# Two-by-two blocks with seven products for the gate and up projections of twenty feature blocks

## The chip, the cores and the metric

One core of one Trainium2 chip runs the whole program. The metric is the device time of one execution in microseconds (us); the kernel before takes 2099.5 us, the median of three runs from 2099.29 to 2100.41 us.

## What is computed

One decoder layer on 1024 tokens of width 1024 in 32-bit floats: a SwiGLU feed-forward of 2816 features, a token mixer (four gated-DeltaNet heads and four gated-linear-attention heads), and a second SwiGLU, each followed by a layer norm. The part that the change touches is the two feed-forwards:

```python
def _swiglu(x, w_gate, w_up, w_down):
    return (jax.nn.silu(x @ w_gate) * (x @ w_up)) @ w_down

x = _layer_norm(ALPHA * x + 0.5 * _swiglu(x, ffn1...), ln1_g, ln1_b)
x = _layer_norm(ALPHA * x + _token_mixer(x, ...), ln2_g, ln2_b)
x = _layer_norm(ALPHA * x + 0.5 * _swiglu(x, ffn2...), ln3_g, ln3_b)
```

## The kernel before, in words

Features are cut into 22 blocks of 128, tokens into two halves of 512, and the width 1024 (over which gate and up sum) into eight slices of 128. Every operand of a large product is kept as two parts, hi and lo (`split`, L120 and L121: ScalarE casts hi, VectorE subtracts to get lo), and each product is three matmuls: hi·hi, hi·lo, lo·hi. So the gate of one block for one half of the tokens (`proj`, L183, L184 and L186) is 8 slices x 3 = 24 matmuls of 128x128 by 128x512 into one PSUM bank. The weights come in two loads of 256 KB per block and matrix (`weight`, L128), into raw tiles `wr` (five of them), and are split into `wh` and `wl` (six pairs).

`hidden` makes a block: gate for each half, Silu on ScalarE (L314), up for each half, the product with the gate on VectorE (L319), and the split of the result. `down` (L205 to L207, L210) multiplies the results of two blocks with their rows of `w_down`: units of one token block of 128 and one half of the columns, 2 x 3 matmuls each into one of three `pd` banks, and VectorE adds the bank to the running sum `acc` in SBUF (L210).

The stages in their order: `ffn_groups(1, ...)` does blocks 0 to 11 of the first feed-forward in pairs for both halves (to about 400 us); inside it `hidden_first` brings in x itself, with `acc` as its staging room, and the constants are loaded after the second pair. `middle` does blocks 12 to 21 of the first feed-forward one half at a time, the first norm, the mixer, the second norm, and blocks 0 to 7 of the second feed-forward, of which half 1 comes last, from about 1500 us. There `ffn` takes the Tanh form of Silu. `ffn_groups(2, ...)` does blocks 8 to 17 in pairs for both halves, and blocks 18 to 21 half by half with the last norm amid them.

All of this is one stream of instructions for each engine. The framework that builds the program puts each engine's instructions in an order of its own, by the order of the text and by when it reckons each to be ready; on the chip each engine then takes its queue in that order. SP issues all loads and stores. The layer norm `ln` (L250 to L257) transposes the rows through `pd`, writes `xf` on ScalarE (L254) and splits it into the parts of x for the next stage.

Of the kernel before, what the change touches and what calls it, by code (L numbers as in the profile page):

```python
# [28 lines left out]
# the rows that the layer norms get here are the reference's over ALPHA  # L29
# [13 lines left out]
BUFS = {"w": 6, "h": 3, "xf": 3, "wr": 5, "f": 4, "g": 6, "raw": 1, "q": 1, "k": 2, "v": 1, "tt": 1, "z": 1, "on": 2, "am": 1, "pt": 1, "qd": 1, "vb": 1,  # L43
        "v0": 1, "v1": 1, "kd": 1, "mi": 1, "ui": 1, "wi": 2}
K1, K2 = 12, 8
LAST = 4
# [35 lines left out]
class Layer:  # L82
    def __init__(self, tc, ctx, a):
        self.tc, self.nc, self.a = tc, tc.nc, a
        pool = lambda name, bufs, **kw: ctx.enter_context(tc.tile_pool(name=name, bufs=bufs, **kw))
        self.cp = pool("cp", 1)
        self.xp = pool("xp", 1)
        self.wp = pool("wp", 1)
        self.sp = pool("sp", 1)
# [6 lines left out]
        self.centred = {}  # L96

# [15 lines left out]

    def xtile(self, half, k):
# [19 lines left out]
    def constants(self):  # L134
        cp, nc = self.cp, self.nc
# [7 lines left out]
        self.mhalf = cp.tile([P, 4], F32, name="mhalf")  # L143
        nc.gpsimd.memset(self.mhalf[:], -0.5)

    def load_constants(self):
# [3 lines left out]
        for j in range(0, MASKW, HT):  # L150
            w = min(HT, MASKW - j)
            raw = self.u("xf", self.wp)
# [8 lines left out]
    def load_x(self, half, k):  # L161
        h, l = self.xtile(half, k)
        c = 4 * half + k // 2
        if k % 2 == 0:
            # acc serves as staging room until it is loaded itself
            self.acc[c] = self.wt(self.xp, [D], f"acc{c}", 1)
# [4 lines left out]
    def load_acc(self, c):  # L171
        t = self.acc[c]
        self.tc.keep_in_program_order(self.nc.sync.dma_start(t[:], self.a["x"][c]))
# [15 lines left out]
    def down(self, hs, ws, half, scale, cs=range(4), sums=None, cuts=((0, HT), (HT, D)), ahead=1):  # L189
        """acc += scale / ALPHA * sum of h w for the half's token blocks cs; sums gets the new acc's sums over the columns."""  # L190
# [3 lines left out]
        while units:  # L194
            # the first few units take all but the last h first, which has just been computed
# [22 lines left out]
    def ln_stats(self, c, cuts=2):  # L218
        nc = self.nc
        acc = self.acc[c]  # L220
        st = self.wt(self.sp, [4, 6], "st", 2)
        mv = self.wt(self.sp, [4], "mv", 3)
# [8 lines left out]
    def ln_row(self, i, d, tags="gb", bufs=1):  # L231
        out = []
        for j in range(2):
            t = self.wt(self.wp, [HT], tags[j], bufs)
# [4 lines left out]
    def ln(self, i, half):  # L239
        """Normalises the half's acc, writes the parts hi and lo of the transpose of LN(acc)."""  # L240
# [5 lines left out]
        for k in range(KB):  # L246
# [6 lines left out]
            xf = self.u("xf", self.wp)  # L253
            nc.scalar.activation(xf[:], ps[:], AF.Identity, bias=bc, scale=gc)  # L254
            self.split(h[:], l[:], xf[:])
# [11 lines left out]
    def out_stats(self, c, sums):  # L267
        """The rows' means and reciprocal deviations; (acc - mean) * g in two temporary tiles."""
# [5 lines left out]
        else:  # L274
            mv, sq = self.wt(self.sp, [4], "mv", 3), self.tiny("sq", 2)
# [11 lines left out]
    def centre(self, c, mv, ds=(0, 1)):  # L287
        for d in ds:
            t = self.centred[c, d] = self.u("xf", self.wp)
# [16 lines left out]
    def gate_silu(self, w, half, tanh):  # L306
        nc = self.nc
        ps = yield from self.proj(w, half)
        s = self.u("xf", self.wp)
# [14 lines left out]
    def hidden(self, idx, f, halves, pool, tags, bufs, tanh=False):  # L324
        """silu(x w_gate) * (x w_up) of one block of features (twice that with tanh), as parts hi and lo."""
# [31 lines left out]
    def ffn(self, idx, fs, half):  # L357
        """The blocks fs of features for one half of the tokens, two at a time."""
        for n in range(0, len(fs), 2):
            hs = []  # L360
            for f in fs[n:n + 2]:
                h = yield from self.hidden(idx, f, (half,), self.wp, ("hh", "hl"), BUFS["h"], True)
                hs.append(h[half])
            ws = [self.weight(self.a[f"wd{idx}"][f]) for f in fs[n:n + 2]]
            yield from self.down(hs, ws, half, 0.25, ahead=AHEAD)

    def ffn_groups(self, idx, groups, first=False, last=()):
        """Blocks of features in groups, both halves of the tokens, while the mixer needs no room."""
        with self.tc.tile_pool(name=self.nm("fx"), bufs=1) as fx:
            for n, fs in enumerate(groups):  # L370
                hs = []
                for f in fs:
                    if first and f == 0:
                        hs.append(self.hidden_first(fx, ("gh", "gl"), BUFS["g"]))
                    else:
                        hs.append(now(self.hidden(idx, f, (0, 1), fx, ("gh", "gl"), BUFS["g"])))
                self.downs_group(idx, fs, hs, (0, 1), fx, first=first and fs[0] == 0)
                if first and n == 1:
                    self.load_constants()
            if last:  # L380
                for half in range(2):
                    hs = [now(self.hidden(idx, f, (half,), fx, ("gh", "gl"), BUFS["g"])) for f in last]
                    self.downs_group(idx, last, hs, (half,), fx, end=True)

    def downs_group(self, idx, fs, hs, halves, fx, first=False, end=False):
        ws = [self.weight(self.a[f"wd{idx}"][f], *((fx, "f") if 2 * n < BUFS["f"] else ())) for n, f in enumerate(fs)]
        if first:
            for c in range(KB):
                self.load_acc(c)
        for half in halves:  # L390
            for c in range(4):
                sums = self.tiny("sums", 2) if end and c < 3 else None
                last = end and half == 1 and c == 3
                work = self.down([h[half] for h in hs], ws, half, 0.5, [c], sums,
                                 ((0, HT), (HT, HT + HT // 2), (HT + HT // 2, D)) if last else ((0, HT), (HT, D)))
                if end:
                    for _ in range(2):
                        next(work)
                    if half or c:
                        self.out_rows(4 * half + c - 1)  # L400
                now(work)
                if end:
                    self.out_stats(4 * half + c, sums)
            if end and half:
                self.out_rows(KB - 1)
# [101 lines left out]
    def finish(self, ons, half, blk, wz, wcol):  # L507
        """Gates heads' normalised outputs [token, dv] and adds their share of w_out."""
        nc = self.nc
        ms = []  # L510
        for n, on in enumerate(ons):
            ps = yield from self.proj(self.weight(self.a["win"][wz + n]), half)
            m = [self.wt(self.wp, [HT], t, BUFS["h"], F32R) for t in ("hh", "hl")]
# [13 lines left out]
    def pull(self, n, skip=0):  # L527
        """Emits about n products of the work that waits, from its entry number skip on."""
# [31 lines left out]
    def gdn(self, h, half, free):  # L560
# [50 lines left out]
        # the inverse of each B0 x B0 diagonal block of I + A, column after column from the last  # L611
# [8 lines left out]
        for j in range(B0 - 1, 0, -1):  # L620
            # row j of each block, in all of the block's partitions
# [14 lines left out]
        for b in LEVELS:  # L636
            # the columns of the second halves of the blocks of 2 * b
# [18 lines left out]
        for b in (32, 64):  # L656
            # block by block, as the halves of the blocks begin at partitions that the engines can start at
# [6 lines left out]
            # over all rows of the block, as the others are zero: all products that write a bank start at the same row  # L664
# [45 lines left out]
    def values(self, ws, half):  # L710
        """The pair's values with the tokens on the partitions: both weights have the columns of both heads, for half of the rows."""
# [47 lines left out]
    def gla(self, p, half, free):  # L759
# [41 lines left out]
        for i, hb in enumerate(GLEVELS):  # L801
# [8 lines left out]
            # the rows of the second halves are masked below, so that any finite numbers serve there  # L810
# [46 lines left out]
    def run(self):  # L857
        self.constants()
        self.halo, self.S, self.SB = {}, [None] * NH, [None] * 2
        self.ffn_groups(1, [range(n, n + 2) for n in range(0, K1, 2)], first=True)  # L860
        with self.tc.tile_pool(name="mp", bufs=1) as self.mp:
            self.middle()
        cut = [*range(K2, NF - LAST, 2), NF - LAST]
        self.ffn_groups(2, [range(a, b) for a, b in zip(cut, cut[1:])], last=range(NF - LAST, NF))

    def middle(self):
# [43 lines left out]
        now(self.ffn(2, range(K2), 1))  # L910
# [69 lines left out]
```

## Time and profile before

| | us |
|---|---|
| median of three runs | 2099.5 |
| span of the profiled execution, first to last instruction | 2097.4 |
| TensorE (PE) busy | 2067.7 |
| VectorE (DVE) busy | 1284.9 |
| ScalarE (ACT) busy | 697.2 |

The profiled execution's own time is its span of 2097.4 us and what lies around it. Against the median this is 2.1 us (2099.5 - 2097.4). In the tables of stretches each engine shows its busy time and, in brackets, the number of its instructions that began there. A matmul's row shows some 0.39 us, but the matmuls overlap: what one costs is the distance between the starts of two.

### The profile page before, as it was taken

How to read it: one execution, taken by the hardware profiler on the slowest of the kernel's cores; microseconds unless marked ns; L12 is line 12 of the kernel's file. 1: busy time of each engine (PE TensorE's matmuls, PEld its weight loads, DVE VectorE, ACT ScalarE, POOL GpSimd, SP SyncE). 2: the span in 40 equal slices, each digit the busy share in tenths (PEclk: the TensorE clock that was granted, in tenths of full speed). 3: DMA queues.
4: the chain of work that ended last, by engine and by line, in shares of the span. 5: the costliest groups of instructions: out<-in, count | busy, mean ns of one | idle time of the engine just before them, and what ended most of it. 6: DMA issues, size and time to landing. Idle time of an engine off the chain costs nothing.

```text
span 2097.4 us, 27456 instructions
## 1 busy us (share of the span) xinstructions
PE 2067.7 (99%) x10292; PEld 1695.0 (81%) x10292; DVE 1284.9 (61%) x2793; ACT 697.2 (33%) x1395; POOL 54.6 (3%) x87
## 2 busy tenths in 40 slices
PE   9999999999999999999999999999999999999998
PEld 7888888888887787788788777888788888888887
DVE  4434333454678888768899887778755333333456
ACT  5211121123254444434464443343422211112232
POOL 0000000000000000000101000001000000000000
PEclk9999999999999999999999999999999999999999
DMA  8111111122222212222131222122323211111232
GB/s 288 49 55 48 43 55 46 46 97 99 89 93 86 71 56 79 70 69 91 66 111 66 71 76 66 66 71 71 121 96 105 80 46 46 51 40 61 76 106 85
DMA packets 87109, 163.03 MB, mean 78 GB/s; under 512 B 10048, under 2 KB 10560, under 8 KB 86976
## 3 DMA queue, kind: packets, MB, share of 16 engines
q1 hardware_dynamic: 86976, 161.29, 22.9%
q8 instruction: 80, 1.31, 0.3%
q14 instruction: 53, 0.43, 0.1%
HBM read 157.06 MB, written 4.19 MB: 77 GB/s over the span
## 4 chain that ended last, share of the span: by engine, by line
PE 87%; DVE 8%; ACT 2%; issue 2%; POOL 1%; DMA 1%; SPq 0%; DVEq 0%; ACTq 0%; POOLq 0%
PE pa L183 17%; PE pa L184 17%; PE pa L186 17%; PE pd L205 8%; PE pd L206 8%; PE pd L207 8%; PE pm L824 1%; PE pm L422 1%; DVE wl L121 1%; DVE acc L210 1%; DVE acc L264 1%; PE pa L724 1%; DVE xl L121 1%; PE pa L725 1%; PE pa L723 1%
## 5 line engine op out<-in xcount | busy, mean ns | idle before, releaser
L183 PE MATMUL pa<-xh,wh 128*128 128x512 f32 x1808 | 716.6, 397 | 8.7 <-ACT xh L120 5.1
L184 PE MATMUL pa<-xl,wh 128*128 128x512 f32 x1808 | 708.7, 392 | 0.1
L186 PE MATMUL pa<-xh,wl 128*128 128x512 f32 x1792 | 704.3, 393 | 0.0
L121 DVE TENSOR_TENSOR wl<-wr,wh 128x512 fp32r<-128x512 f32 (+1 forms) x489 | 334.1, 686 | 350.9 <-ACT wh L120 340.9
L120 ACT CAST wh<-wr 128x512 fp32r<-128x512 f32 (+1 forms) x489 | 302.6, 621 | 709.5 <-PE pa L184 482.9
L183 PEld LDWEIGHTS pa<-xh,wh 128*128 128x128 f32 x1808 | 340.5, 188 | 80.0 <-ACT xh L120 5.9
L184 PEld LDWEIGHTS pa<-xl,wh 128*128 128x128 f32 x1808 | 340.3, 188 | 68.0 <-DVE xl L121 1.8
L186 PEld LDWEIGHTS pa<-xh,wl 128*128 128x128 f32 x1792 | 337.2, 188 | 67.9
L210 DVE SCALAR_TENSOR_TENSOR acc<-pd,acc 128x512 f32<-128x512 f32 x433 | 293.8, 687 | 125.4 <-PE pd L207 122.0
L205 PE MATMUL pd<-wh,hh 128*128 128x512 f32 x416 | 165.4, 404 | 2.2 <-ACT xf L254 1.4
L206 PE MATMUL pd<-wl,hh 128*128 128x512 f32 x416 | 164.2, 396 | 0.1
L207 PE MATMUL pd<-wh,hl 128*128 128x512 f32 x416 | 162.1, 395 | 0.0
L319 DVE TENSOR_TENSOR xf<-xf,pa 128x512 f32<-128x512 f32 x88 | 60.4, 686 | 165.8 <-PE pa L186 165.8
L206 PE MATMUL pd<-fl,gh 128*128 128x512 f32 (+1 forms) x386 | 150.0, 389 | 0.0
L205 PE MATMUL pd<-fh,gh 128*128 128x512 f32 (+1 forms) x386 | 150.0, 389 | 0.0
L207 PE MATMUL pd<-fh,gl 128*128 128x512 f32 (+1 forms) x386 | 149.8, 388 | 0.0
L205 PEld LDWEIGHTS pd<-wh,hh 128*128 128x128 f32 x416 | 78.1, 188 | 24.2 <-ACT hh L120 5.1
L120 ACT CAST fh<-wr 128x512 fp32r<-128x512 f32 x52 | 32.2, 622 | 195.4 <-PE pd L207 165.6
L207 PEld LDWEIGHTS pd<-wh,hl 128*128 128x128 f32 x416 | 78.1, 188 | 17.7 <-DVE hl L121 2.9
L206 PEld LDWEIGHTS pd<-wl,hh 128*128 128x128 f32 x416 | 78.3, 188 | 13.9 <-DVE wl L121 0.8
L205 PEld LDWEIGHTS pd<-fh,gh 128*128 128x128 f32 x386 | 72.5, 188 | 15.2
L207 PEld LDWEIGHTS pd<-fh,gl 128*128 128x128 f32 x386 | 72.5, 188 | 15.2
(251 smaller groups left out, 1987.5 us busy)
## 6 DMA issues: line engine op xcount, KB each, us to landing
wr<-gu SPq DMA_DIRECT2D x263, 256.0 KB, 2.5
wr<-wd SPq DMA_DIRECT2D x132, 256.0 KB, 2.6
wr<-win SPq DMA_DIRECT2D x116, 256.0 KB, 2.6
wr<-wout SPq DMA_DIRECT2D x32, 256.0 KB, 2.5
acc<-xT SPq DMA_DIRECT2D x16, 256.0 KB, 5.4
acc<-x SPq DMA_DIRECT2D x8, 512.0 KB, 8.7
out_dram<-acc SPq DMA_DIRECT2D x7, 512.0 KB, 2.6
g<-lnrow SPq DMA_DIRECT2D x9, 256.0 KB, 3.4
```

What stands on the lines that cost most here:

```text
L120: self.nc.scalar.copy(hi, src)
L121: self.nc.vector.tensor_tensor(lo, src, hi.bitcast(F32), ALU.subtract)
L183: nc.tensor.matmul(ps[:], hi[:, sl], xh[k][:], start=(k == 0), stop=False)
L184: nc.tensor.matmul(ps[:], hi[:, sl], xl[k][:], start=False, stop=(lo is None and k == KB - 1))
L186: nc.tensor.matmul(ps[:], lo[:, sl], xh[k][:], start=False, stop=(k == KB - 1))
L205: nc.tensor.matmul(p, hh[:, sl], wh[:, ds], start=(i == 0), stop=False)
L206: nc.tensor.matmul(p, hh[:, sl], wl[:, ds], start=False, stop=False)
L207: nc.tensor.matmul(p, hl[:, sl], wh[:, ds], start=False, stop=(i == n - 1))
L210: nc.vector.scalar_tensor_tensor(acc, p, scale / ALPHA, acc, ALU.mult, ALU.add, accum_out=None if sums is None else sums[:, d:d + 1])
L264: nc.vector.tensor_tensor(acc, acc, g[:], ALU.mult)
L319: self.nc.vector.tensor_tensor(s[:], s[:], ps[:], ALU.mult)
L422: self.nc.tensor.transpose(self.chunk(ps, c), s, self.ident)
```

## The change

For ten pairs of feature blocks (2 to 11 of the first feed-forward, 8 to 17 of the second) gate and up are each taken as a product of two-by-two blocks: two halves of the tokens, two halves of the width, two blocks of features. Instead of the eight block products (each 4 slices x 3 matmuls) seven are made, from sums of blocks: x keeps four kinds of sums for the whole stage (`token_sums`, `last_sums`; three in a new pool, the fourth in the room of half 1's own first four slices), the weights' sums are made for each pair (`weight_sums`), and the results are put together from two PSUM banks with three copies to SBUF and three additions for each matrix (`project`). `w_down` stays as it was, but its 16 units for a pair now stand among the seven gate products of the next pair (`TURNS`: g gate, d down, u up). The parts of weights are asked for four products ahead (`DEEP`).

Because one kind of sums takes the room of a part of x, that part is loaded again afterwards (`restore`); because the second stage needs x after the norm, `ln` now stores it to DRAM (`x2d`, 16 stores of 256 KB). The constants are loaded at the start of `middle`. Half 1 of blocks 0 to 7 of the second feed-forward moves behind `middle` and takes Silu in place of Tanh. `wr` has seven tiles in place of five.

```diff
-BUFS = {"w": 6, "h": 3, "xf": 3, "wr": 5, "f": 4, "g": 6, ...
+BUFS = {"w": 6, "h": 3, "xf": 3, "wr": 7, "f": 4, "g": 6, "gs": 4, "sn": 3, ...
+PRODUCTS = (("P1", 0), ("P2", 1), ("P6", 0), ("P5", 1), ("P7", 0), ("P4", 0), ("P3", 1))
+TURNS = "ggddddgddddgddddgddddgguuuuuuu"
+DEEP = 4
 def ln(self, i, half):
             nc.scalar.activation(xf[:], ps[:], AF.Identity, bias=bc, scale=gc)
+            if i:
+                x = self.x2d[half, k] = self.dp.tile([P, HT], F32, ...)
+                nc.sync.dma_start(x[:], xf[:])
+    def token_sums(self, q):
+        s1, a22, s2, s4 = [self.load(self.raw_x(i, 4 * j + q)) for i, j in ((1, 0), (1, 1), (0, 0), (0, 1))]
+        tt(s1[:], s1[:], a22[:], ALU.add)
+        tt(s2[:], s1[:], s2[:], ALU.subtract)
+        tt(s4[:], s4[:], s2[:], ALU.subtract)
+        for n, t in (("P6", s2), ("P5", s1), ("P3", s4)):
+            self.sum_parts(n, q, t)
+    def last_sums(self):
+        for q in range(KB // 2):
+            s3, a21 = [self.load(self.raw_x(i, q)) for i in range(2)]
+            self.nc.vector.tensor_tensor(s3[:], s3[:], a21[:], ALU.subtract)
+            self.sum_parts("P7", q, s3)
+    def weight_sums(self, order, b11, b12, b21, b22):
+        t11, t21 = load(b11), load(b21)
+        yield parts(t11)
+        t12, t22 = load(b12), load(b22)
+        yield parts(t21)
+        t2 = self.u("wr", self.wp)
+        tt(t11[:], t12[:], t11[:], ALU.subtract)
+        tt(t2[:], t22[:], t11[:], ALU.subtract)
+        yield parts(t2)
+        yield parts(t11)
...
+    def project(self, ops, hid, up):
...
+        for n, b in PRODUCTS:
+            yield
+            ps = banks[b]
+            for q, (xh, xl) in enumerate(self.tokens(n)):
+                new = n in ("P1", "P2", "P5") and q == 0
+                nc.tensor.matmul(ps[:], op[0][:, sl], xh[:], start=new, ...)
+                nc.tensor.matmul(ps[:], op[0][:, sl], xl[:], start=False, ...)
+                nc.tensor.matmul(ps[:], op[1][:, sl], xh[:], start=False, ...)
+            if n in ("P1", "P6", "P5"):
+                keep(n, ps)
+            elif n == "P2":
+                done("11", (kept["P1"], ps))
+            elif n == "P7":
+                done("22", (kept["P5"], ps))
+            elif n == "P3":
+                done("12", (kept["P6"], ps))
+            else:
+                done("21", None)
 def run(self):
-        self.ffn_groups(1, [range(n, n + 2) for n in range(0, K1, 2)], first=True)
+            hs = [self.hidden_first(self.fx, ("gh", "gl"), 4)]
+            for q in range(KB // 2):
+                self.token_sums(q)
+            hs.append(now(self.hidden(1, 1, (0, 1), self.fx, ("gh", "gl"), 4)))
+            for c in range(KB):
+                self.load_acc(c)
+            self.last_sums()
+            self.ffn_pairs(1, range(2, K1), (0, {...}))
...
+            for q in range(KB // 2):
+                now(self.ffn(2, range(q * K2 // 4, (q + 1) * K2 // 4), 1, True))
+                self.token_sums(q)
+            self.last_sums()
+            self.ffn_pairs(2, range(K2, NF - LAST))
+        self.last_blocks(range(NF - LAST, NF))
```

`keep` is a ScalarE copy of a bank to SBUF; `done` adds that copy to a bank on VectorE and goes on with Silu (gate) or with the multiplication and the split (up).

## Rows read from the trace of the kernel before

**Rows 1.** The page's first part: busy us, share of the span and instructions of each engine.

```profile
PE 2067.7 (99%) x10292; PEld 1695.0 (81%) x10292; DVE 1284.9 (61%) x2793; ACT 697.2 (33%) x1395; POOL 54.6 (3%) x87
```

**Rows 2.** Busy time by stretch, in us: the pairs of the first feed-forward, the mixer, and a stretch of the pairs of the second. The last three columns are the granted clock, the share of the 16 DMA engines and GB/s.

```profile
12.00:402.00 390.00, 390.00 (x1720) 322.69 (x1719) 153.73 (x231) 83.26 (x137) 0.99 (x3) 1.00 0.21 73
500.00:1500.00 1000.00, 983.27 (x5528) 801.64 (x5527) 805.65 (x2041) 432.07 (x951) 47.10 (x65) 1.00 0.24 78
1700.00:1800.00 100.00, 100.00 (x442) 82.76 (x441) 31.09 (x47) 19.33 (x32) 0.00 (x0) 1.00 0.15 52
```

**Rows 3.** TensorE in order of time in the first feed-forward, start and duration in us: the first and the last of 97 rows in a row, across the turn from `down` to `proj`.

```profile
59.66 0.39 PE L205 MATMUL pd<-fh,gh 128*128 128x512 f32 x1
...
81.45 0.39 PE L183 MATMUL pa<-xh,wh 128*128 128x512 f32 x1
```

**Rows 4.** VectorE in order of time where it has no idle time between: start and duration in us.

```profile
73.36 0.68 DVE L210 SCALAR_TENSOR_TENSOR acc<-pd,acc 128x512 f32<-128x512 f32 x1
73.96 0.68 DVE L121 TENSOR_TENSOR fl<-wr,fh 128x512 fp32r<-128x512 f32 x1
74.56 0.68 DVE L210 SCALAR_TENSOR_TENSOR acc<-pd,acc 128x512 f32<-128x512 f32 x1
```

**Rows 5.** The page's costliest groups, those of VectorE and ScalarE: busy us and the mean ns of one, and the idle time of the engine before them.

```profile
L121 DVE TENSOR_TENSOR wl<-wr,wh 128x512 fp32r<-128x512 f32 (+1 forms) x489 | 334.1, 686 | 350.9 <-ACT wh L120 340.9
L120 ACT CAST wh<-wr 128x512 fp32r<-128x512 f32 (+1 forms) x489 | 302.6, 621 | 709.5 <-PE pa L184 482.9
L210 DVE SCALAR_TENSOR_TENSOR acc<-pd,acc 128x512 f32<-128x512 f32 x433 | 293.8, 687 | 125.4 <-PE pd L207 122.0
L319 DVE TENSOR_TENSOR xf<-xf,pa 128x512 f32<-128x512 f32 x88 | 60.4, 686 | 165.8 <-PE pa L186 165.8
```

**Rows 6.** TensorE in order of time at a `down` right behind the `proj` that makes its last operand, in the one-half form of `ffn`.

```profile
422.24 0.39 PE L186 MATMUL pa<-xh,wl 128*128 128x512 f32 x1
...
423.82 0.74 PE L205 MATMUL pd<-wh,hh 128*128 128x512 f32 x2
424.40 0.39 PE L206 MATMUL pd<-wl,hh 128*128 128x512 f32 x1
424.63 0.40 PE L205 MATMUL pd<-wh,hh 128*128 128x512 f32 x1
424.86 0.42 PE L207 MATMUL pd<-wh,hl 128*128 128x512 f32 x1
```

**Rows 7.** VectorE in order of time at the same place: the product with the gate, with its wait, and the lo part made of it.

```profile
422.66 0.69 DVE L319 TENSOR_TENSOR xf<-xf,pa 128x512 f32<-128x512 f32 x1 [1.56 <-PE pa L186]
...
424.04 0.69 DVE L121 TENSOR_TENSOR hl<-xf,hh 128x512 fp32r<-128x512 f32 x1
```

**Rows 8.** SP's issues at the start, in order of time: start, time on the queue, count.

```profile
7.70 5.24 SPq L168 DMA_DIRECT2D acc<-xT  x8
13.36 2.34 SPq L128 DMA_DIRECT2D wr<-gu  x4
```

**Rows 9.** VectorE at the start, in order of time: the last parts of x, the lo part of block 0's first result, the first lo parts of block 1's weights, and the last product of block 0.

```profile
20.31 1.29 DVE L121 TENSOR_TENSOR xl<-acc,xh 128x512 fp32r<-128x512 f32 x2
21.51 0.69 DVE L121 TENSOR_TENSOR gl<-xf,gh 128x512 fp32r<-128x512 f32 x1
22.11 1.89 DVE L121 TENSOR_TENSOR wl<-wr,wh 128x512 fp32r<-128x512 f32 x3
...
30.58 0.69 DVE L319 TENSOR_TENSOR xf<-xf,pa 128x512 f32<-128x512 f32 x1 [1.59 <-PE pa L186]
```

**Rows 10.** The page's DMA issues: KB each, and median us from issue to landing.

```profile
wr<-gu SPq DMA_DIRECT2D x263, 256.0 KB, 2.5
...
out_dram<-acc SPq DMA_DIRECT2D x7, 512.0 KB, 2.6
```

**Rows 11.** Busy time by stretch at the start, columns as in Rows 2.

```profile
8.00:10.00 2.00, 2.00 (x5) 1.45 (x6) 1.82 (x4) 1.64 (x4) 0.00 (x0) 1.00 1.05 389
...
15.00:20.00 5.00, 5.00 (x24) 4.15 (x23) 4.00 (x7) 4.30 (x9) 0.00 (x0) 1.00 1.05 387
```

**Rows 12.** TensorE in order of time in its first us of work.

```profile
8.41 0.63 PE L186 MATMUL pa<-xh,wl 128*128 128x512 f32 x1
8.83 0.63 PE L183 MATMUL pa<-xh,wh 128*128 128x512 f32 x1
...
10.97 0.52 PE L186 MATMUL pa<-xh,wl 128*128 128x512 f32 x1
11.34 0.39 PE L183 MATMUL pa<-xh,wh 128*128 128x512 f32 x1
```

**Rows 13.** ScalarE in order of time in the norm that closes the mixer: two of `ln`'s rows and their casts, a cast of weights, and the next two rows.

```profile
1470.43 1.45 ACT L254 ACTIVATE xf<-pd,lncol 128x512 f32<-128x512 f32 x2 [2.47 <-PE pd L250]
1471.78 1.13 ACT L120 CAST xh<-xf 128x512 fp32r<-128x512 f32 x2
1472.81 0.62 ACT L120 CAST wh<-wr 128x512 fp32r<-128x512 f32 x1
1473.33 1.45 ACT L254 ACTIVATE xf<-pd,lncol 128x512 f32<-128x512 f32 x2
```

**Rows 14.** Who waited for whom, longest first: us in total, times, longest us.

```profile
ACT wh L120 <- PE pa L184: 482.9, 269, 23.0
```

More of the change, by code (lines that the diff above doesn't have):

```diff
@@ L112, in tiny, with phase @@
         return self.wt(self.sp, [w], tag, 2)
+    def phase(self, name, side=None):
+        return self.tc.tile_pool(name=self.nm(name), bufs=1, reuse_waits="tile")
     def xtile(self, half, k):
@@ L132, in weight, with constants @@
         return out
-    def constants(self):
-        cp, nc = self.cp, self.nc
+    def constants(self, cp):
+        nc = self.nc
         self.cst = cp.tile([P, C_END], F32, name="cst")
@@ L355, in hidden_first, with ffn @@
         return hs
-    def ffn(self, idx, fs, half):
-        for n in range(0, len(fs), 2):
+    def ffn(self, idx, fs, half, out=False):
+        pool, tags, n = (self.fx, ("gh", "gl"), 4) if out else (self.hp, ("hh", "hl"), BUFS["h"])
+        for i in range(0, len(fs), 2):
             hs = []
-            for f in fs[n:n + 2]:
-                h = yield from self.hidden(idx, f, (half,), self.wp, ("hh", "hl"), BUFS["h"], True)
+            for f in fs[i:i + 2]:
+                h = yield from self.hidden(idx, f, (half,), pool, tags, n, not out)
@@ L363, in ffn @@
                 hs.append(h[half])
[L364 to L405, printed above, removed]
+            ws = [self.weight(self.a[f"wd{idx}"][f]) for f in fs[i:i + 2]]
@@ new lines, in ffn, with last_blocks, last_downs @@
+            yield from self.down(hs, ws, half, 0.5 if out else 0.25, ahead=AHEAD)
+    def last_blocks(self, fs):
+        with self.phase("ep") as fx:
+            self.hp = fx
+            self.scr = "xf", fx
+            for k in range(KB // 2):
+                self.restore(1, k)
+            for half in range(2):
+                hs = [now(self.hidden(2, f, (half,), fx, ("gh", "gl"), BUFS["g"])) for f in fs]
+                self.last_downs(fs, hs, half, fx)
+    def last_downs(self, fs, hs, half, fx):
+        ws = [self.weight(self.a["wd2"][f], *((fx, "f") if 2 * n < BUFS["f"] else ())) for n, f in enumerate(fs)]
+        for c in range(4):
+            sums = self.wt(self.sl, [2], "sums", 2) if c < 3 else None
+            last = half == 1 and c == 3
+            work = self.down([h[half] for h in hs], ws, half, 0.5, [c], sums,
+                             ((0, HT), (HT, HT + HT // 2), (HT + HT // 2, D)) if last else ((0, HT), (HT, D)))
+            for _ in range(2):
+                next(work)
+            if half or c:
+                self.out_rows(4 * half + c - 1)
+            now(work)
+            self.out_stats(4 * half + c, sums)
+        if half:
+            self.out_rows(KB - 1)
@@ new lines, in down_turns, with halves_of @@
+    def down_turns(self, ops, hid):
+        for d in range(2):
+            for i in range(2):
+                for c in range(4):
+                    yield
+                    hs = [hid[f"{i + 1}1"], hid[f"{i + 1}2"]]
+                    ws = [{d: ops[n, d]} for n in range(2)]
+                    now(self.down(hs, ws, i, 0.5, [c], cuts=((d * HT, (d + 1) * HT),)))
+    def halves_of(self, blocks):
+        for d in range(2):
+            for b in blocks:
+                raw = self.u("wr", self.wp)
+                self.nc.sync.dma_start(raw[:], b[:, HALVES[d]])
+                hl = [self.wt(self.wp, [HT], "w" + e, BUFS["w"], F32R) for e in "hl"]
+                self.split(hl[0][:], hl[1][:], raw[:])
+                yield hl
@@ L909, in middle @@
             self.drain(t)
-        now(self.ffn(2, range(K2), 1))
 def now(work):
```

161 lines of the change are left out of this document (139 added, 22 removed).

## The prediction

> **What bounds the kernel now.** I read the page's first part first: TensorE is busy 99% of the span, VectorE 61%, ScalarE 33% [rows 1]. These shares mix stages, so next come the stretches [rows 2]: in the pairs of both feed-forwards TensorE has no idle time at all, VectorE is busy 39% and 31% and the DMA engines 15 to 21%; in the mixer TensorE lacks 17 us of 1000 and VectorE is at 81%. A row of a matmul overlaps the next, so its 0.39 us is not its price. The price is the distance between starts: 81.45 - 59.66 us over 96 steps is 0.227 us [rows 3], and 390 us over 1720 matmuls gives the same [rows 2]. The change works in the stretches where every matmul is on the path, so a matmul left out there is worth 0.227 us until some other wait takes its place.
>
> **What is taken away.** A pair has, for each of gate and up, 8 block products of 12 matmuls; 7 remain. That is 24 matmuls less in a pair of 288, and 240 in ten pairs: 240 x 0.227 = **54.4 us**. The `down` matmuls and all others stay.
>
> A page of the Trainium skill would give another sum: "TensorE: Matmul & The Clock Gate", section "Back-to-back issue gap", has about 131 ns as the sustained step of matmuls with 512 columns. By it the 240 would be worth 31 us, and the forecast below would be some 23 us higher. The trace does not agree: its step is 0.227 us over whole stretches, and I give that sum no chance.
>
> **What a pair gets more of.** I count VectorE's instructions in the text. Before: 12 lo parts of weights, 4 products with the gate, 4 lo parts of results, 16 additions to `acc`, 36 in all. After: 18 lo parts of weights (7 + 7 + 4) with 8 sums, 6 additions from PSUM, 4 products, 4 lo parts, 16 additions to `acc`: 56. One starts 0.60 us behind the other [rows 4], though its row shows 0.69 us [rows 5]: 33.6 us of the pair's 264 x 0.227 = 59.9 us. ScalarE goes from 20 to 32 (6 casts and 6 copies more) at 0.62 us [rows 5], 19.8 us. Both are hidden behind matmuls on the mean. The densest place is the up stretch: 84 matmuls, 19.1 us, against 20 VectorE instructions by the text's order (9 for coming weights, 11 for results), 12 us. Hidden too; a single product (2.7 us) has room for four instructions, and the text asks for five at P2 and at most four elsewhere. If that cover were gone, each VectorE instruction in front would cost 0.6 us. DMA: 12 loads of 256 KB for a pair, as before.
>
> **The bank that two products share.** P1, P6, P7 and P4 go to one bank, P2, P5 and P3 to the other. In most places another product or four `down` units lie between a result's reading and the next write to its bank: 2.7 us, against one copy or addition. In the up stretch P7 and P4 are neighbours in the same bank, so P4's first matmul waits for VectorE's addition; likewise in the gate of the first pair of the second stage, which has no `down` units. That is 11 places. Bare price: VectorE starts 0.03 us after the matmul's end [rows 6, 7], so 0.39 + 0.03 + 0.69 - 0.227, or 0.9 us, up to 1.0 with the way back, and 1.6 behind one more instruction. But P3, in the other bank, is ready then, and TensorE's queue is not in the text's order: where the last operand of a `down` was late, matmuls of other units were put in front, and two steps took 0.58 us in place of 0.45 [rows 6]. So 0 to 1.6 us for each place, and I take the 0.13 us of that row, it being the same kind of place: **1.4 us**. The ends of the two stages, where `down` follows the last up directly, are such places as well, with one addition more than in the row: 0 to 0.7 us each, I take **0.3 us** for both.
>
> **The start.** Here I expect most of what is lost. The token sums bring 16 loads of 256 KB which stand in the text ahead of block 1's weights, and the raw tiles are seven. Before, those weights were issued at 13.4 us, right behind x [rows 8]; now the seven tiles go to sums, and block 1's first raw tile is the 17th, for which ten must have been given back. A slice of sums takes six VectorE instructions and gives back one tile after its first and one after each of its last three; the tenth comes with the 16th instruction. VectorE is through with x at about 21.5 us [rows 9]; 16 x 0.6 us and one product of block 0 in between make 31.7 us. Then 2.5 us to land [rows 10] and 0.62 us for the cast: 34.8 us. Block 0 ends at 30.6 us [rows 9], and nothing else is ready, so TensorE idles 4.2 us, and some 0.6 us more for the first lo part, which is queued behind the last sums. After so long an idle time the matmuls may be slow for a while: in the first us of work they stood 0.42 us apart, nearly the factor between 2.4 and 1.2 GHz, though the granted clock of the stretch says 1.00 [rows 11, 12]; from 8.41 to 11.34 us that is seven steps, 1.3 us too long. I take 1.2 us. Sum: **6.0 us**. Bounds: 0, if the builder's order lets block 1's weights through first; 10.3, if all 24 instructions of the sums, the product and the lo part (26 x 0.6 us from 21.5) go ahead of the load, landing, cast and lo part (37.1 + 2.5 + 0.6 + 0.7, less 30.6).
>
> The same page, section "Part 1: The HAM clock gate", says that an idle TensorE falls back to 1.2 GHz and that matmuls after a pause run at that level first. The spacing agrees, the granted clock column does not.
>
> **Behind it on SP's queue**: block 1's four loads, `acc` (8 x 512 KB) and eight loads for the last sums, some 7 MB at 390 GB/s [rows 11], 18 us from 32 us on; the first pair needs its weights at 30.6 + 6 + 96 x 0.227 = 58 us. Hidden by block 1. The last sums hold four of the seven raw tiles until block 1's last product has read the part of x that they replace, so the first pair's fourth raw tile comes late: 0 to 3 us, I take **0.5 us**, since 48 matmuls (10.9 us) stand before its use.
>
> **Other edges.** The norm that feeds the second stage now stores `xf`, of which there are three tiles. Two of its rows with their casts take 2.9 us of ScalarE [rows 13]; a tile bound by 0.73 us of writing and 2.6 us of landing [rows 10] is back after 3.3 us, so three tiles allow one row each 1.1 us, no limit; with one tile held by a gate's result 1.7 us in place of 1.45, 0.2 x 8 for a norm. Two norms: 0 to 3.5 us, I take **1 us**. Restoring x (8 loads and splits) and the constants lie under the 96 `down` matmuls that close a stage (21.8 us); without that cover some 6 us each, for landing and four splits. Silu for Tanh in half 1 saves 8 VectorE instructions beside a full TensorE: nothing. Two more raw tiles in the mixer and a new order there: -3 to +3 us, taken as 0.
>
> **Sum** against the profiled execution: 2097.4 - 54.4 + 1.4 + 0.3 + 6.0 + 0.5 + 1.0 = 2052.2 us of span, and with the 2.1 us that the median lies above the span **2054 us**.
>
> **The rivals.**
> *The sums cost nothing at the start*: block 1's weights pass, 6 us less, 2048 us. For it: the DMA engines are full only to about 20 us [rows 11]. Against: the raw tiles go by the text's order. 0.12.
> *The bank of P7 and P4 is waited for in full*, because the builder reckons VectorE's addition to be quicker than it is, or VectorE has an instruction in front: 11 x 1.0 to 1.6 in place of 1.4 us, 2064 to 2070 us. Against: rows 6. 0.18.
> *ScalarE's queue blocks the banks* (the other side). ScalarE stands at the head of its queue, blocked by a cast that waits until a product gives back its pair `wh`, `wl`, for 483 us in 269 waits, 1.8 us each [rows 14]. Before, nothing urgent lay behind. Now the copies of P1 and P6 do, and the product two places on waits for them. If such a cast is queued ahead of the copy, the copy comes with the end of the following product, and TensorE stands for up to a product: 2.7 us at two places of each up and two of each gate (where `down` units hide it). With the up stretches alone, 20 x 2.7 = 54 us, the gain is gone, and with the 9 us of edges the time is 2108 us. It decides from the point where the copy is more than 2.7 us behind its product's end at both places. Against: parts are asked for four products ahead, and six pairs of tiles make a cast wait for the very product whose copy follows. In full 0.07; at one of the two places, 2081 us, 0.05.
> *It does not do what it says*: as much TensorE time appears elsewhere (operands late all through a pair, 5 us a pair), 2099 to 2103 us: 0.03.
>
> **How the numbers follow.** The forecast, 2048 to 2060 us, has 0.55. The range takes in most of the first rival and all of the second, and the bounds of the start (2048 to 2058) with those of the mixer: 2044 to 2078 us, leaving out some 0.18. A measurement of this kernel can tell about 0.2% (4.2 us) from no change. Faster by more: 0.55 + 0.12 + 0.18 + 0.05 = 0.90; within: 0.03; slower by more: 0.07.
>
> **What would show it.** PE with 240 instructions less, at steps of 0.227 us in the pairs; VectorE at about 60% there; TensorE idle for 4 to 6 us around 31 us, ended by ScalarE's cast of block 1's weights; P3's matmuls ahead of P4's in the up stretches. I am wrong if TensorE's idle time in a pair exceeds 1 us, if it waits for ScalarE's copies, or if the step of the matmuls grows with VectorE's load.

## The result, and the profile after

The changed kernel takes 2079.45 us, the median of four runs from 2077.97 to 2080.24 us, beside 2099.39 us for the kernel before on the same chip: a ratio of 0.990, interval 0.9886 to 0.9914. The forecast was 2054 us with a range of 2044 to 2078. So the sign was right, the gain is 20 us in place of 45, and the time lies 1.5 us above the range. The profiled execution's span is 2075.8 us, where the sum of the prediction said 2052.2: 23.6 us are to be found.

The page's first part, busy us, share and instructions by engine:

```profile
PE 2039.1 (98%) x10052; PEld 1651.6 (80%) x10052; DVE 1443.4 (70%) x3057; ACT 785.9 (38%) x1553; POOL 54.8 (3%) x87
```

Against [rows 1] TensorE has exactly 240 instructions less, VectorE 264 more. The count of the work was right. Next the stretches of [rows 2], in the same columns, and one of the first feed-forward's pairs alone:

```profile
12.00:402.00 390.00, 383.78 (x1646) 309.88 (x1645) 238.37 (x373) 130.54 (x222) 2.34 (x9) 0.99 0.30 95
100.00:200.00 100.00, 100.00 (x432) 80.70 (x432) 58.35 (x90) 32.88 (x56) 0.00 (x0) 1.00 0.18 56
500.00:1500.00 1000.00, 983.50 (x5502) 797.99 (x5501) 804.31 (x2038) 430.32 (x947) 47.11 (x65) 1.00 0.26 81
1700.00:1800.00 100.00, 100.00 (x432) 80.73 (x431) 60.60 (x94) 33.73 (x57) 0.00 (x0) 1.00 0.20 58
```

Two things are to be seen. In the pairs TensorE is busy all the time, at the full granted clock, and still begins 432 matmuls in 100 us where the kernel before began 442 (in [rows 2] for the second stage; the first has the same count): nobody makes it wait, each matmul has become dearer. And the first stretch lacks 6.2 us of TensorE's time, which is the start.

The dearer matmuls, in order of time in the up stretch of a pair (rows left out in between are all single matmuls): 24 with x as the streamed tile, then 24 with the sums P6 and P5, then 12 with the sums P7, which lie in the room of a part of x and go by its tiles' name, then the sums P3.

```profile
102.84 0.39 PE L528 MATMUL pm<-xh,wh 128*128 128x512 f32 x1
...
108.30 0.40 PE L528 MATMUL pm<-P60h,wh 128*128 128x512 f32 x1
...
113.91 0.40 PE L528 MATMUL pm<-xh,wh 128*128 128x512 f32 x1
...
116.64 0.40 PE L528 MATMUL pm<-P30h,wh 128*128 128x512 f32 x1
```

The first 24 steps take 5.46 us, 0.2275 each, near the price of [rows 3]; the next 24 take 5.61 us, 0.2338 each; the 12 of P7 take 2.73 us, 0.2275 each. It is the same instruction throughout, with weights from the same pool, and P7 shows that sums as such are not dear. But VectorE is busier beside the dear 24 (the third busy time, 5.31 us against 1.98), so these rows alone do not tell the place of the streamed tile from VectorE's load:

```profile
102.84:108.30 5.46, 5.46 (x26) 4.51 (x24) 1.98 (x3) 2.36 (x4) 0.00 (x0) 1.00 0.25 89
108.30:113.91 5.61, 5.61 (x25) 4.52 (x24) 5.31 (x9) 2.34 (x4) 0.00 (x0) 1.00 0.00 0
```

The duration column shows 0.39 or 0.40 in both and would hide the difference.

The start, TensorE in order of time and then the granted clock by stretch (columns as above):

```profile
29.94 0.39 PE L192 MATMUL pa<-xh,wl 128*128 128x512 f32 x1
36.36 0.79 PE L189 MATMUL pa<-xh,wh 128*128 128x512 f32 x1 [6.03 <-ACT wh L131]
36.95 0.63 PE L190 MATMUL pa<-xl,wh 128*128 128x512 f32 x1
...
40.93 0.55 PE L192 MATMUL pa<-xh,wl 128*128 128x512 f32 x1
41.31 0.39 PE L189 MATMUL pa<-xh,wh 128*128 128x512 f32 x1
```

```profile
35.00:40.00 5.00, 3.64 (x8) 2.66 (x9) 4.92 (x9) 3.87 (x7) 0.00 (x0) 0.50 0.90 270
40.00:45.00 5.00, 5.00 (x21) 4.04 (x20) 0.56 (x1) 0.07 (x1) 0.00 (x0) 0.88 1.00 392
```

The pause is 6.2 us beyond a normal step, ended by ScalarE's cast of block 1's weights. Behind it 11 steps take 4.95 us in place of 2.50, at a granted clock of 0.50, that is 1.2 in place of 2.4 GHz. SP's queue says why (start, time on the queue, count), to be read against [rows 8]:

```profile
13.29 17.05 SPq L429 DMA_DIRECT2D wr<-xT  x16
32.42 2.74 SPq L139 DMA_DIRECT2D wr<-gu  x4
```

The 16 loads for the sums stand on the queue for 17 us, waiting for raw tiles, and block 1's weights are issued behind them, as the prediction had it.

### The profile page after: what moved, and what is told of

It is laid out like the page before. It is cut to its first block, busy times and chain, and to the rows that moved or that the text cites. A ratio compares the mean times of both kernels' runs of the same rounds, so it can differ in the third digit from the quotient of the medians.

```text
span 2075.8 us, 27622 instructions
## 1 busy us (share of the span) xinstructions
PE 2039.1 (98%) x10052; PEld 1651.6 (80%) x10052; DVE 1443.4 (70%) x3057; ACT 785.9 (38%) x1553; POOL 54.8 (3%) x87
## 4 chain that ended last, share of the span: by engine, by line
PE 87%; DVE 7%; ACT 2%; issue 2%; DMA 1%; POOL 1%; SPq 0%; DVEq 0%; ACTq 0%; POOLq 0%
PE pa L189 11%; PE pa L190 11%; PE pa L192 11%; PE pd L212 9%; PE pd L211 9%; PE pd L213 9%; PE pm L528 3%; PE pm L529 3%; PE pm L530 3%; PE pa L529 3%; PE pa L528 3%; PE pa L530 3%; PE pm L1019 1%; PE pm L617 1%; DVE wl L132 1%
## 5 line engine op out<-in xcount | busy, mean ns | idle before, releaser
L189 PE MATMUL pa<-xh,wh 128*128 128x512 f32 x1168 | 469.5, 402 | 15.0 <-ACT wh L131 6.0
L190 PE MATMUL pa<-xl,wh 128*128 128x512 f32 x1168 | 462.1, 396 | 0.1
L192 PE MATMUL pa<-xh,wl 128*128 128x512 f32 x1152 | 456.2, 396 | 0.0
L189 PEld LDWEIGHTS pa<-xh,wh 128*128 128x128 f32 x1168 | 221.2, 189 | 62.8 <-ACT wh L131 6.7
L190 PEld LDWEIGHTS pa<-xl,wh 128*128 128x128 f32 x1168 | 221.1, 189 | 43.7 <-DVE xl L132 1.8
L192 PEld LDWEIGHTS pa<-xh,wl 128*128 128x128 f32 x1152 | 217.2, 189 | 43.8 <-DVE wl L132 0.5
L211 PE MATMUL pd<-wh,gh 128*128 128x512 f32 (+1 forms) x450 | 176.9, 394 | 1.2 <-ACT gh L131 1.0
L212 PE MATMUL pd<-wl,gh 128*128 128x512 f32 (+1 forms) x450 | 178.1, 396 | 0.0
L213 PE MATMUL pd<-wh,gl 128*128 128x512 f32 (+1 forms) x450 | 176.6, 393 | 0.0
L211 PEld LDWEIGHTS pd<-wh,gh 128*128 128x128 f32 x450 | 84.5, 188 | 23.4 <-ACT gh L131 2.2
```

Of the source, the lines that this page charges most:

```text
L189: nc.tensor.matmul(ps[:], hi[:, sl], xh[k][:], start=(k == 0), stop=False)
L190: nc.tensor.matmul(ps[:], hi[:, sl], xl[k][:], start=False, stop=(lo is None and k == KB - 1))
L192: nc.tensor.matmul(ps[:], lo[:, sl], xh[k][:], start=False, stop=(k == KB - 1))
L211: nc.tensor.matmul(p, hh[:, sl], wh[:, ds], start=(i == 0), stop=False)
L212: nc.tensor.matmul(p, hh[:, sl], wl[:, ds], start=False, stop=False)
L213: nc.tensor.matmul(p, hl[:, sl], wh[:, ds], start=False, stop=(i == n - 1))
```

## The addresses: what told the theories apart

The trace gives a start for each matmul, the built program the address of each tile within a partition of SBUF (the on-chip memory that holds the operands). Put side by side, the distance from a matmul to the next goes with one quantity: the address of the tile that it streams, less the address of the weight tile that is loaded next, taken modulo 256. Here are the remainders of the tiles' own addresses (all tiles of a name have the same) and the steps that differ among the matmuls with 512 columns:

```
                x   weights wh,wl   sums P..   results g   differing steps
before         128       128           -           96           119 of 7626
after          160       160          64           64          2999 of 7386
gap of 32      160       160          96           96          3000
gap of 96      160       160         160          160             7
before + 32    128       160           -          128          5300 of 7626
```

In the kernel before, `down` streamed tiles of `w_down` named `f`, which lay at the remainder of the results that it loads as weights (both 96), `proj` streamed x against weights of the same remainder, and so did the half-by-half form of `down` (results `hh` 128, like the weights): nearly every step was an equal one. The change takes `w_down` into the weights' tiles (`wh`, `wl`) and its results and sums into pools that begin elsewhere, so `down` (a difference of 96) and the products with sums (160) differ. The section on the change says that `w_down` stays as it was: that holds for its values and not for its tiles. Mean steps in ns by that difference, 100 to 375 us, from the starts of the trace (60 to 375 us for before; steps under 0.3 us, their number in brackets):

```
difference   0: 226.8 (before, 1379)    228.2 (after, 449)   226.9 (gap of 96, 1200)
difference  96: 233.6 (after, 404)      160: 233.8 (after, 323)
difference  64: 230.3 (gap of 32, 407)  192: 233.4 (gap of 32, 323)
difference 128: 233.0 (gap of 224, 730)
difference  32: 233.3 (gap of 64, 400), 235.0 (before, 4)
difference 224: 233.5 (gap of 64, 323), 235.0 (before, 5)
```

The nine differing steps of before (4 and 5) also tell which weights count. They stand at turns from `proj` to `down`, where the matmul's own weights lie at the remainder of its streamed tile and only the next ones do not.

In the experiments theory A is that of the addresses, first with remainders modulo 64. Its rivals put the dearer step down to what runs beside TensorE, VectorE's load above all, or to what its own work consists of; neither is touched by an unused tile of some bytes. An address can be moved alone: a tile of a few bytes ahead of the pools shifts them, and the order of TensorE's matmuls in the built program stays what it was. Each ratio below is to the kernel before on the same chip, where that took 2099.4 to 2101.3 us.

**A gap of 32 bytes in the changed kernel.**

```diff
 def run(self):
...
     self.nc.gpsimd.memset(self.mhalf[:], -0.5)
+    self.nc.gpsimd.memset(self.sl.tile([P, 8], F32, name="gap")[:], 0.0)
```

> The kernel after with one unused tile of 32 bytes ahead of the pools of the sums, the results and the mixer, so that the tiles that TensorE streams and those it loads as weights start at addresses with the same remainder by 64 everywhere. Theory A (a matmul's step grows from 0.227 to 0.234 us when the streamed tile and the tile of the next weight load differ in that remainder): 2989 of the 2996 such steps go, times 6.8 ns is 20.3 us, so 2059 us. Theory B (the step grows because VectorE, busier than before, disturbs TensorE): VectorE's load is the same, so 2079.5 us, and the step in the pairs stays at 0.232 us. Theory C (the step grows because consecutive products take turns in PSUM banks and TensorE's order is more mixed): 2079.5 us as well.

Measured: 2070.77 us (2069.96 to 2071.89), ratio 0.9857 [0.9842, 0.9872]. An empty tile of 32 bytes makes the changed kernel 8.7 us faster, which no rival allows, but that is less than half of what A had said. Modulo 256 the differences are now 64 and 192, not 0: the theory had the right quantity and the wrong modulus.

**The same gap in the kernel before**, ahead of the weights' pool.

```diff
 def constants(self):
...
+    nc.gpsimd.memset(self.wp.tile([P, 8], F32, name="gap")[:], 0.0)
```

> The kernel before with one unused tile of 32 bytes at the head of the pool of the weights, nothing else: x stays where it was, the weights' tiles move by 32 bytes against it. Theory A: steps with differing remainders go from 119 to 5299, times 6.8 ns is 35 us, so 2135 us, with the step of the projections at 0.234 us and that of the down matmuls of the pairs at 0.227. Theories B and C: no engine does anything else than before, so 2099.4 us.

Measured: 2127.36 us (2126.87 to 2128.44), ratio 1.0128 [1.0111, 1.0145]. Nothing of the change is in this kernel, and it is 27 us slower, where A had said 35 and its rivals nothing. Its `proj` is now the dear one; TensorE in order of time, 45 steps of 0.2333 us apart:

```profile
80.45 0.40 PE L184 MATMUL pa<-xh,wh 128*128 128x512 f32 x1
...
90.95 0.40 PE L184 MATMUL pa<-xh,wh 128*128 128x512 f32 x1
```

It also excludes that the streamed tile's own alignment is what counts: x stays at 128, and its matmuls turn dear because the weights have moved.

**Gaps of 64, 96 and 224 bytes**, the same line with 16, 24 and 56 elements.

> The kernel after with a gap of 64 bytes in the place of the first run's 32. Theory A: the remainders by 64 are those of the kernel after, so 2079.5 us. If instead any shift of these pools mattered (the distance to something else, or a change in the order of the instructions): like the first run, some 2059 us.

> The kernel after with a gap of 96 bytes: streamed tile and next weights now have the same remainder by 256 in all but 7 large matmuls (in the first run, with 32 bytes, they still differed by 64 in 2294 steps of 0.2304 us and by 192 in 699 of 0.2334 us). Theory A, with 256 or 128 in place of 64: every step in the pairs back at 0.227 us, 2297 x 6.8 ns and 699 x 7.0 ns less than after, 20.5 us, so 2059 us. Theory B (VectorE's load, which stays at some 60% in the pairs) and C (turns of banks): the step stays above 0.230 us and the time at 2071 us or more.

> The kernel after with a gap of 224 bytes: 2993 steps differ by 128 in the remainder by 256, all others by nothing. If the remainder by 128 is what counts: 2059 us as with 96 bytes, steps of 0.227 us. If the remainder by 256: steps of 0.230 to 0.234 us where they differ, 2069 to 2080 us.

Measured: 2079.74 us with 64 bytes (ratio 0.9897 [0.9883, 0.9912]), 2062.58 us with 96 (0.9821 [0.9804, 0.9837]), 2077.59 us with 224 (0.9892 [0.9877, 0.9907]). Only the gap that makes the differences 0 takes the whole loss away. The gap of 64 adds the same instruction as the one of 32 and gains nothing, so the tile as such does not help. With 224 the differences are 128 and the step stays dear, so an equal remainder modulo 128 is not enough. Whether the modulus is 256 or 512 stays open: in all of these programs the equal pairs lie a multiple of 512 bytes apart, and none a multiple of 512 and 256 more. With 96 bytes, two of the stretches shown above, and the same place in the up stretch:

```profile
12.00:402.00 390.00, 383.45 (x1674) 314.76 (x1674) 241.17 (x377) 132.98 (x226) 2.34 (x9) 0.99 0.29 97
100.00:200.00 100.00, 100.00 (x441) 82.25 (x440) 59.03 (x91) 32.75 (x56) 0.00 (x0) 1.00 0.18 58
```

```profile
103.27 0.39 PE L528 MATMUL pm<-xh,wh 128*128 128x512 f32 x1
...
108.71 0.39 PE L528 MATMUL pm<-P60h,wh 128*128 128x512 f32 x1
...
114.15 0.39 PE L528 MATMUL pm<-xh,wh 128*128 128x512 f32 x1
```

```profile
108.71:114.15 5.44, 5.44 (x25) 4.50 (x24) 5.13 (x9) 2.27 (x4) 0.00 (x0) 1.00 0.00 0
```

Both groups of 24 take 5.44 us, 0.2267 a step, and VectorE is busy for 5.13 us beside the second, close to the 5.31 of before the gap. Over the 100 us it begins 91 instructions and is busy for 59.03 us, against 90 and 58.35 in the kernel after. Its load is the same, so the load is not the cause.

## The start, and what is left

**Block 1 ahead of the sums.** In the text `hidden(1, 1)` moves ahead of the loop of `token_sums`.

```diff
     hs = [self.hidden_first(self.fx, ("gh", "gl"), 4)]
+    hs.append(now(self.hidden(1, 1, (0, 1), self.fx, ("gh", "gl"), 4)))
     for q in range(KB // 2):
         self.token_sums(q)
-    hs.append(now(self.hidden(1, 1, (0, 1), self.fx, ("gh", "gl"), 4)))
```

> The kernel after with the token sums behind block 1 in the text, so that block 1's weights are loaded ahead of the sums' 16 loads. Theory (the sums' loads hold the raw tiles, and TensorE idles 6.2 us and then runs twelve matmuls at half clock, 2.3 us more): 8.5 us less, 2071 us. Rival (the wait only moves: the sums then come late for the first pair, or x2 and acc loads get in each other's way): a new wait of TensorE around 60 to 70 us, and 2074 to 2080 us.

Measured: 2078.23 us (2076.22 to 2081.83), ratio 0.9894 [0.9879, 0.9909], not to be told from the change itself. The pause has moved; TensorE, and SP's queue:

```profile
52.87 0.39 PE L192 MATMUL pa<-xh,wl 128*128 128x512 f32 x1
59.28 0.80 PE L528 MATMUL pa<-xh,wh 128*128 128x512 f32 x1 [6.02 <-ACT wh L131]
```

```profile
43.01 11.46 SPq L429 DMA_DIRECT2D wr<-xT  x8
55.59 2.73 SPq L459 DMA_DIRECT2D wr<-gu  x4
```

Now the eight loads of the last sums hold the queue, for raw tiles that come back only when block 1 has read the part of x that they replace, and the first pair's weights stand behind them.

**Both queues and the gap.** `last_sums` is called from inside the first pair (at its third turn, ahead of the product that needs it), block 1 stays ahead of the sums, and the gap is 96 bytes.

```diff
-        for make, asked in turns:
+        for turn, (make, asked) in enumerate(turns):
+            if sums and turn == 2:
+                self.last_sums()
...
-            self.last_sums()
-            self.ffn_pairs(1, range(2, K1), (0, {...}))
+            self.ffn_pairs(1, range(2, K1), (0, {...}), True)
```

> The 96-byte gap, the token sums behind block 1 in the text, and the last sums behind the first two products of the first pair, so that neither block 1's weights nor the first pair's stand behind the sums' loads. In the earlier run with the token sums alone moved, the pause of 6.2 us and the slow matmuls behind it moved from 30 to 53 us, as the first pair's weights then stood behind eight loads whose raw tiles are held. Theory (the raw tiles go by the text's order): no pause of over 1 us before 100 us, 8.5 us less than with the gap alone, 2050 us. Rival (the first 60 us are bound by the bytes to be loaded, some 21 MB at 0.39 MB a us): a pause of several us comes back at a third place, 2055 to 2060 us.

Measured: **2051.23 us** (2048.34 to 2051.85), ratio 0.9762 [0.9747, 0.9776]. SP issues block 1's weights at 13.53 us, and the pause is gone at both places; the turn to the first pair costs some tenths:

```profile
13.53 2.41 SPq L139 DMA_DIRECT2D wr<-gu  x4
16.29 20.81 SPq L429 DMA_DIRECT2D wr<-xT  x16
...
42.40 4.18 SPq L459 DMA_DIRECT2D wr<-gu  x4
```

```profile
52.48 0.39 PE L192 MATMUL pa<-xh,wl 128*128 128x512 f32 x1
52.76 0.50 PE L528 MATMUL pa<-xh,wh 128*128 128x512 f32 x1
```

**The smaller terms**, each on top of that kernel: P3 ahead of P4 in the list of products; with that, the last of the second stage's token sums one call earlier; and, on the kernel of 2051.23 us alone, the norm's stores left out, with the first input read in place of what they stored.

```diff
-PRODUCTS = (... ("P7", 0), ("P4", 0), ("P3", 1))
+PRODUCTS = (... ("P7", 0), ("P3", 1), ("P4", 0))
```

> The version with 96 bytes of gap and the later sums (2051.2 us), with P3 put ahead of P4 in the list of products, so that no two products that stand side by side write the same PSUM bank. Theory of the shared bank (0.2 us at each of the nine places where P4 began behind P7, and some tenths at the two stage ends): 2048.5 to 2049.5 us, TensorE's distances between starts at those places back at 0.227 us. Rival, that the 0.2 us are the price of something else, as the text's order of reads: unchanged at 2051 us. Second rival, that P3 behind P7 makes the sums for block product 12 late in VectorE's queue: slower, 2053 us or more.

```diff
-                self.token_sums(q)
+                for s in ((0,), (1,), (2, 3), ())[q]:
+                    self.token_sums(s)
```

> As the kernel with P3 ahead of P4, and in the second stage the token sums of slices 2 and 3 both stand behind the third call of the feed-forward, none behind the fourth. Theory that the pause of 2.0 us near 1598 us comes from VectorE's queue being filled with the last token sums: 1 to 2 us less than that kernel, about 2047 us, and no pause over 1 us at the turn to the pairs. Rival, that the restores and the last sums fill the queue by themselves: the same within 0.5 us.

```diff
 def ln(self, i, half):
...
-                nc.sync.dma_start(x[:], xf[:])
...
 def raw_x(self, i, k):
-        return self.x2d[i, k][:] if self.x2d else self.a["xT"][i, k]
+        return self.a["xT"][i, k]
```

> The version with 96 bytes of gap and the later sums (2051.2 us), without the norm's stores of x to DRAM: the token sums and the restores of the second feed-forward read the first input instead of the norm's result, so that the operands of the second feed-forward's sums are other numbers, with all loads and arithmetic in place. Prediction's term for the stores, 1 us (bounds 0 to 3.5): 2050 us. Rival, that the stores hold up the norm by the tile xf that they bind and explain the 2.5 us that the mixer is still slower by: 2048.5 us. Second rival, that they cost nothing: 2051 us.

Measured: 2052.99 us (ratio 0.9768 [0.9755, 0.9782]), 2050.07 us (0.9756 [0.9743, 0.9769]) and 2049.68 us (0.9754 [0.9738, 0.9769]). With the 0.9762 of the kernel that they start from, the intervals overlap: these times cannot tell the kernels apart, and only the traces, of one execution each, say something. In the changed kernel P4 begins behind P7 like this, with P3's first matmuls in between (second stage, TensorE):

```profile
1643.54 0.39 PE L530 MATMUL pa<-P30h,wl 128*128 128x512 f32 x1
1643.77 0.40 PE L528 MATMUL pa<-P31h,wh 128*128 128x512 f32 x1
1644.09 0.50 PE L528 MATMUL pa<-xh,wh 128*128 128x512 f32 x1
1644.42 0.40 PE L529 MATMUL pa<-xl,wh 128*128 128x512 f32 x1
```

Two steps of 0.32 and 0.33 us: 0.2 us for the place. With P3 first, the turn into P3 and the one into P4 are ordinary steps:

```profile
1641.87 0.39 PE L530 MATMUL pm<-xh,wl 128*128 128x512 f32 x1
1642.10 0.39 PE L528 MATMUL pm<-P30h,wh 128*128 128x512 f32 x1
...
1644.59 0.39 PE L530 MATMUL pm<-P33h,wl 128*128 128x512 f32 x1
1644.82 0.39 PE L528 MATMUL pm<-xh,wh 128*128 128x512 f32 x1
```

There are nine such places. In the kernel of 2051.23 us they cost 1.9 us over ordinary steps; with P3 first no step between the pairs' products is over 0.25 us. From the first product to the last, the first stage takes 299.0 us in place of 300.4 and the second 277.2 in place of 278.5. This bears out the shared bank; the whole kernel's time does not show the gain.

With the sums earlier, a pause still stands ahead of the second stage's pairs:

```profile
1598.98 0.39 PE L212 MATMUL pd<-wl,gh 128*128 128x512 f32 x1
1600.76 0.50 PE L211 MATMUL pd<-wh,gh 128*128 128x512 f32 x1 [1.39 <-ACT gh L131]
```

It is 1.6 us longer than a step, and 1.7 with the sums in their place: where the token sums stand is not its cause. That the last sums and the restored x make it by themselves, as the rival has it, fits and was not tried.

The stores show in one pause at the end of the mixer, where `down` waits for the lo part of its weights. Here it is in the kernel of 2051.23 us, and then the same matmul without the stores:

```profile
1467.18 0.50 PE L212 MATMUL pd<-wl,hh 128*128 128x512 f32 x1 [1.01 <-DVE wl L132]
```

```profile
1466.32 0.47 PE L212 MATMUL pd<-wl,hh 128*128 128x512 f32 x1
```

All nine kernels with the stores have this pause, 1.00 to 1.01 us of idle time; the kernel before, with its gap or without, and the one without the stores do not. The pause just ahead of it ranges from 0.6 to 1.1 us with the stores and is 0.6 without, so it says nothing of them. The stored x is first loaded again behind the pause, at 1480 us, so the loads do not make it. Whether the stores' own time does, or the order that the builder gives VectorE with them, stays open.

## Why the prediction was off, step by step

The failed step is the price of a matmul. The prediction took 0.227 us from [rows 3] and let it stand for every matmul of the changed kernel. What the runs showed in its place: 2999 of 7386 steps stand at some 234 ns because of where their tiles lie, and that is 17.1 of the 23.6 us. The prediction named the one way it saw for its price to break, "if the step of the matmuls grows with VectorE's load"; the step did grow, but by the place of the tiles. The rows of before hardly show it, since there the remainders were equal everywhere but in 119 steps; the nine of those in the first pairs stood at 235 ns, and what was special about these could have led there. The whole diff does say that `w_down`, x's sums and the results change their pools.

Of the 23.6 us, by spans of profiled executions:

| term | forecast | measured | from |
|---|---|---|---|
| 240 matmuls at 0.227 us | -54.4 | -54.4 | reckoned: 10292 to 10052 instructions; 226.9 ns with equal remainders |
| addresses | 0 | +17.1 | 2075.8 less 2058.7, the gap of 96 |
| start and first pair | 6.5 | +8.9 | 2058.7 less 2049.8, the sums later |
| bank, stage ends, stores, mixer | 2.7 | +6.8 | 2049.8 less (2097.4 - 54.4) |

The measured terms are differences of single executions, and those of one kernel lie up to 3.5 us apart. By the medians of the runs the last three are 16.9, 11.4 and 6.2 us.

**Addresses.** The 17.1 us are the larger part of the miss, with a check from the stretches: 1646 matmuls against 1674 with the gap from 12 to 402 us are 28 x 0.227 = 6.4 us for one stage's pairs. Set matmul against matmul, the pairs of the two stages make 6.1 and 6.2 us of it. Another 4.5 us lie between the two and 1.6 in the last blocks, at matmuls that the prediction had as staying what they were; the start, 1.3 us longer with the gap, takes some off.

**The start** was the right mechanism with a size too small: a pause of 6.2 us for 4.8 (the weights issued at 32.4 us for 31.7, and TensorE up again 3.9 us later for 3.7, while block 0 ended at 30.3 for 30.6), and 2.45 us of half clock for 1.2. The tenth raw tile came back with the 16th of VectorE's instructions for the sums, as reckoned; it ends at 32.39 us, and SP issues at 32.42:

```profile
31.71 0.68 DVE L132 TENSOR_TENSOR P62l<-wr,P62h 128x512 fp32r<-128x512 f32 x1
```

The Trainium skill, "TensorE: Matmul & The Clock Gate", section "Part 1: The HAM clock gate", has a paused TensorE come back at 1.2 GHz. The prediction had found spacing and clock column at odds on that; here the trace agrees in both, with steps of mostly 0.42 to 0.43 us and a granted clock of 0.50.

**The bank** was right in kind and size: P3's matmuls ran ahead, 0.2 us a place where 0.13 was taken, at nine places of the eleven, 1.8 us for 1.4. The rival of a full wait is refuted by the rows at 1643 us.

**ScalarE's queue** did not block the banks: TensorE is busy for all of the 100 us in the pairs. The rival "it does not do what it says" came nearest in form, as much time appearing elsewhere in a pair; its cause, late operands, was not there.

**The rest** was 6.8 us for 2.7. Found in the trace of the kernel with the gap and the later sums: 1.9 us at the bank, 0.4 at the first pair, 1.8 ahead of the second stage's pairs (0.7 with the gap alone), and 1.7 more than before in the pauses at the end of the mixer, 1.0 of it in the pause that comes with the stores (1 us was forecast for them). For the start of the second stage the prediction had no term. The remaining 1.0 us is below what single executions of before differ by, and stays open.

## What to carry to other kernels

The price of a matmul that was read from one kernel did not hold in another where the tiles had changed their places: before a count of instructions is multiplied by a step, compare the addresses, modulo 512, of streamed tiles and of the weights loaded behind them. An unused tile of some bytes is a cheap experiment, in both directions. A load moved ahead of another on SP's queue brings its wait for a free tile with it, so look at who stands behind it, and then again at who stands behind that.

## What the runs showed of the hardware that was not expected

A matmul of 128x128 by 128x512 begins 226.9 ns after the one before where the addresses of the streamed tile and of the next weights differ by a multiple of 512 bytes, and 230.3 to 233.8 ns after it where they differ, modulo 256, by 32, 64, 96, 128, 160, 192 or 224 (235 in the few of before); 64 is the mildest with 230.3. A difference of 256 did not occur. What in the chip does it was not tried and stays open. The granted clock showed 1.00 in the first us, at steps of 0.42 us [rows 11, 12], and 0.50 behind the pause at 36 us, at the same steps: the steps are the surer sign.
